# Reciprocal square roots of a single column on VectorE: a Newton step of two instructions with per-partition scalars instead of three

## The chip, the cores and the metric

The kernel runs on one core of one Trainium2 chip. Its engines work side by side from their own instruction queues: TensorE (PE, with its weight loads shown apart as PEld), VectorE (DVE), ScalarE (ACT), GpSimd (POOL) and SyncE (SP), which issues most of the transfers from memory. The metric is the device time of one execution in microseconds (us); lower is better.

## What is computed

The reference is a two-layer decoder trunk for 512 tokens of width 2048, in float32. Layer 0 is gated differential attention with 8 heads, layer 1 a gated RWKV-7 mixer. The change touches layer 0 alone, where each head normalises its attention output row by row:

```python
o = causal_diff_attention(q, k, v, lam)            # (B, T, 8 heads, 256)
o = rms_norm(o, subln_w) * (1.0 - lambda_init)     # y * rsqrt(mean(y*y) + 1e-6) over the 256
o = o.reshape(B, T, DA_WIDTH) * jax.nn.silu(gate)
return o @ w_out
```

The reciprocal root of that `rms_norm` is one number per token and head.

## The kernel before

Every large product is made of three float32r matmuls: each operand is split into a high part (a copy by ACT, `wh`) and a low part (a subtraction by DVE, `wl`), and `mm3` (its matmul is line 118) adds high*high, low*high and high*low. A weight block arrives by DMA in `wraw` (three buffers) or `T`; ACT casts one 128x512 slab of it (line 619) and DVE subtracts (line 620); four buffers hold the split slabs that PE reads. So PE, ACT and DVE form a pipeline that runs a few slabs ahead of the matmuls.

Layer 0 works head by head. While the projections of head h are multiplied (`Seven.head`), the attention of head h-1 runs as a `Chain`: a generator whose pieces are placed between the matmuls of the projection. For each block t of 128 tokens (four blocks a head) it has the pieces `scores`, `turn` (a transposition of the weights), `weigh` and `turn_y`. In `weigh`, PE makes the 128x256 output `o`; ACT squares and sums it into one column `so` (line 435); DVE adds epsilon (436), calls `rsqrt` with n = 1, multiplies the root `ro` with two other columns (439) and writes `y` (440), the normalised and gated 128x256 block. A fixed number of matmuls later PE transposes `y` into `yt` (`turn_y`, line 445), and ACT copies that to `yT` (line 449). PE's queue is in order: if `y` is not there by then, all matmuls behind wait.

`rsqrt` starts from the well-known integer estimate (two instructions, lines 63 and 64) and refines it with three Newton steps of three instructions each (lines 67, 68, 70). It is called 32 times with one column (8 heads x 4 blocks, line 438), and elsewhere with 2, 4, 8 or 16 columns.

Beside the chain, DVE has other work of the head in the same stretch: the rotary embedding of block t of the projected q and k (`rope`, lines 310 to 313, which overwrite the scratch tile `t2` that ACT's four squares of line 302 also write), and the sums of partial products (`take`, line 662). In the last pass it also splits rows of the finished attention for the output projection (lines 474 and 475).

The order of the instructions on every engine is set by a scheduler in the tile framework, from priorities that the code gives and the scheduler's own estimate of when each instruction can start. An instruction more or fewer can therefore change where its neighbours stand. Each engine then runs its list in order, and waits on semaphores where an operand is another instruction's result, also of the same engine.

Of the kernel before, what the change touches and what calls it, by code (L numbers as in the profile page):

```python
# [13 lines left out]
F32 = mybir.dt.float32  # L14
# [4 lines left out]
ALU = mybir.AluOpType  # L19
# [4 lines left out]
P = 128  # L24
# [33 lines left out]
def rsqrt(g, out, v, n, tag):  # L58

    nc = g.nc  # L60
    sh = g.small.tile([P, n], I32, name="rs_i", tag=tag + "i")
    t = g.small.tile([P, n], F32, name="rs_t", tag=tag + "t")
    nc.vector.tensor_single_scalar(sh[:], v.bitcast(I32), 1, ALU.logical_shift_right)
    nc.vector.tensor_scalar(sh[:], sh[:], -1.0, float(0x5F3759DF), ALU.mult, ALU.add)
    y = sh[:].bitcast(F32)
    for i in range(3):
        nc.vector.tensor_mul(t[:], y, y)
        nc.vector.scalar_tensor_tensor(t[:], t[:], -0.5, v, ALU.mult, ALU.mult)
        o = out if i == 2 else y
        nc.vector.scalar_tensor_tensor(o, t[:], 1.5, y, ALU.add, ALU.mult)  # L70
# [245 lines left out]
def norm_qk(g, q):  # L316

    nc, ss, rr = g.nc, q.ss, q.rr
    nc.vector.tensor_scalar(ss[:], ss[:], 1.0 / P, EPS, ALU.mult, ALU.add)
    rsqrt(g, rr[:].rearrange("p t c -> p (t c)"), ss[:].rearrange("p t c -> p (t c)"), 4 * NT, "r16")  # L320
    nc.vector.tensor_mul(rr[:], rr[:], g.rstd0[:, :, None].to_broadcast([P, NT, 4]))
    nc.vector.tensor_scalar(q.sq[:], rr[:, :, 0:2], P ** -0.5, None, ALU.mult)
    for t in range(NT):
        for c in (2, 3):
            cs = slice(c * P, (c + 1) * P)
            nc.scalar.activation(q.t1s[t][:, cs], q.t1s[t][:, cs], AF.Copy, scale=rr[:, t, c : c + 1])
# [57 lines left out]
def attention(g, h, qkT, qkL, sq, vg, gap, rows=None, yT=None):  # L384
# [42 lines left out]
    def weigh(t):  # L427
        b = blocks[t]
        o = g.ps.tile([P, 512], F32, name="o", tag="pc")
        for i in range(t + 1):  # L430
            bs = slice(i * P, (i + 1) * P)
            mm3(nc, o[:, :256], b.at[:, bs], b.al[:, bs], V[:, i, :], VL[:, i, :], i == 0, i == t)
        b.y = w.tile([P, 256], F32, name="y", tag="y", bufs=1)
        so = g.small.tile([P, 1], F32, name="so", tag="so")
        nc.scalar.activation(b.y[:], o[:, :256], AF.Square, scale=b.r[:, 0:1], accum_out=so[:])
        nc.vector.tensor_scalar(so[:], so[:], 1.0 / 256, EPS, ALU.mult, ALU.add)
        ro = g.small.tile([P, 1], F32, name="ro", tag="ro")
        rsqrt(g, ro[:], so[:], 1, "r1")
        nc.vector.scalar_tensor_tensor(ro[:], ro[:], b.r[:, 0:1], g.hrstd0[:, t : t + 1], ALU.mult, ALU.mult)
        nc.vector.scalar_tensor_tensor(b.y[:], o[:, :256], ro[:], G[:, t, :], ALU.mult, ALU.mult)  # L440
# [421 lines left out]
def layer0(g, aps):  # L862
# [3 lines left out]
    with ExitStack() as cx:  # L866
# [68 lines left out]
        g.rstd0 = g.const.tile([P, NT], F32, name="rstd0")  # L935
        g.hrstd0 = g.const.tile([P, NT], F32, name="hrstd0")
        rsqrt(g, g.rstd0[:], ss[:], NT, "r4")
        nc.vector.tensor_scalar(g.hrstd0[:], g.rstd0[:], 0.5, None, ALU.mult)
        with tc.issue_after(g.made[9][0]), tc.issue_after(g.made[9][1]):
# [937 lines left out]
```

## Time and profile before

| | |
|---|---|
| Time, median of 3 runs | 2086.14 us (2085.65 to 2088.14) |
| Time of the profiled execution | 2087.84 us |
| Its span, first to last instruction | 2086.1 us |
| PE busy | 2067.0 us (99%) |
| DVE busy | 1664.8 us (80%), 4353 instructions |
| ACT busy | 1250.9 us (60%) |
| POOL busy | 406.2 us (19%) |
| Attention of layer 0 beside the projections | about 125 to 790 us of the span |

A row of a timeline reads: start in us, duration in us, engine, line, operation, output<-inputs with their sizes, and in brackets how long the engine stood idle before and what ended that. Tile names leave their numbers out. A row of the groups reads: number of instructions, busy us in total, mean ns of one, and idle us before them. A matmul's row lasts longer than its place in the queue: rows of 128x512 start 0.23 us apart and last 0.39 us, since they are pipelined.

### The profile page before, as it was taken

What the parts mean: (1) busy time and instruction counts of PE and PEld (TensorE: products, weight loads), DVE (VectorE), ACT (ScalarE), POOL (GpSimd) and SP (SyncE); (2) the same over time, 40 slices, a digit from 0 to 9 for tenths busy, and PEclk for the clock granted to TensorE, in tenths of its full rate; (3) what the DMA queues carried; (4) which work ended last, traced back from release to release, by engine and by line L of the source; (5) the groups of instructions that cost most, each with busy time, mean ns of one, the idle gap of its engine ahead of it and who ended that gap; (6) DMA issues with size and microseconds to landing.
All of it is one profiled execution on the core that took longest, in us unless ns stands there. A gap on an engine that the chain in (4) does not pass through costs nothing.

```text
span 2086.1 us, 35354 instructions
## 1 busy us (share of the span) xinstructions
PE 2067.0 (99%) x12008; PEld 1708.6 (82%) x12008; DVE 1664.8 (80%) x4353; ACT 1250.9 (60%) x3005; POOL 406.2 (19%) x716
## 2 busy tenths in 40 slices
PE   9999999999999999999999999999999999999999
PEld 8888888888888888888778888888888888877887
DVE  5978778787877886576888888888888888887745
ACT  5766665666666664455666666666666666655333
POOL 0111011111111000101233332233333332342001
PEclk9999999999999999999999999999999999999999
DMA  6576777777777766742212222222222222235665
GB/s 200 146 181 178 182 187 190 181 193 180 190 175 192 182 222 196 169 118 93 79 64 79 80 78 69 82 79 82 76 79 79 79 79 74 89 126 166 204 163 120
DMA packets 101782, 280.71 MB, mean 135 GB/s; under 512 B 12545, under 2 KB 29073, under 8 KB 101601
## 3 DMA queue, kind: packets, MB, share of 16 engines
q1 hardware_dynamic: 68064, 198.90, 29.1%
q0 software_dynamic: 19104, 63.55, 16.4%
q10 hardware_dynamic: 14432, 16.01, 2.2%
q8 instruction: 94, 1.54, 0.3%
q14 instruction: 88, 0.71, 0.1%
HBM read 262.42 MB, written 15.99 MB: 133 GB/s over the span
## 4 chain that ended last, share of the span: by engine, by line
PE 92%; DVE 5%; ACT 2%; issue 1%; DMA 0%; POOL 0%; ACTq 0%; DVEq 0%; POOLq 0%
PE pp L118 70%; PE pt L118 6%; PE gp L1366 1%; PE sc L118 1%; PE sm L1585 1%; PE o L118 1%; PE sm L1607 1%; PE lora L118 1%; PE sm L1598 1%; PE z L118 1%; PE Y L1631 1%; DVE wl L110 1%; PE pt L359 1%; PE pt L1426 1%; PE px L1493 0%
## 5 line engine op out<-in xcount | busy, mean ns | idle before, releaser
L118 PE MATMUL pp<-hH,wh 128*128 128x512 f32 x1024 | 416.9, 407 | 0.0
L118 PE MATMUL pp<-hL,wh 128*128 128x512 f32 x1024 | 412.5, 403 | 0.0
L118 PE MATMUL pp<-hH,wl 128*128 128x512 f32 x1024 | 412.0, 402 | 0.0
L109 ACT CAST wh<-wraw 128x512 fp32r<-128x512 f32 (+1 forms) x412 | 253.8, 617 | 200.5 <-PE pp L118 103.5
L110 DVE TENSOR_TENSOR wl<-wraw,wh 128x512 fp32r<-128x512 f32 (+1 forms) x412 | 286.3, 696 | 102.6 <-ACT wh L109 98.7
L118 PE MATMUL pp<-wh,hH 128*128 128x512 f32 x932 | 366.5, 393 | 0.0
L118 PE MATMUL pp<-wh,hL 128*128 128x512 f32 x932 | 366.5, 393 | 0.0
L118 PE MATMUL pp<-wl,hH 128*128 128x512 f32 x932 | 364.4, 391 | 0.0
L118 PEld LDWEIGHTS pp<-hH,wh 128*128 128x128 f32 x1024 | 192.9, 188 | 37.6 <-issue 1.8
L118 PEld LDWEIGHTS pp<-hH,wl 128*128 128x128 f32 x1024 | 193.2, 189 | 32.8
L118 PEld LDWEIGHTS pp<-hL,wh 128*128 128x128 f32 x1024 | 193.3, 189 | 31.2
L118 PEld LDWEIGHTS pp<-wh,hL 128*128 128x128 f32 x932 | 175.1, 188 | 35.9
L118 PEld LDWEIGHTS pp<-wl,hH 128*128 128x128 f32 x932 | 175.2, 188 | 35.3 <-DVE wl L620 0.2
L118 PEld LDWEIGHTS pp<-wh,hH 128*128 128x128 f32 x932 | 175.3, 188 | 34.2
L620 DVE TENSOR_TENSOR wl<-wraw,wh 128x512 fp32r<-128x512 f32 x224 | 152.4, 688 | 60.0 <-ACT wh L619 59.4
L619 ACT CAST wh<-wraw 128x512 fp32r<-128x512 f32 x224 | 138.2, 620 | 93.8 <-PE pp L118 66.6
L1593 POOL COPY SA<-VS 64x64 f32<-64x64 f32 x224 | 75.1, 335 | 522.8 <-DVE VS L1611 466.4
L118 PE MATMUL pp<-wh,S 128*128 128x512 f32 x504 | 162.1, 395 | 0.0
L1459 DVE SCALAR_TENSOR_TENSOR tmpl<-LT,n,Tm 128x60 f32<-128x60 f32 (+24 forms) x496 | 135.6, 273 | 13.3
L582 POOL DMA_DIRECT2D T<-in_da_w_in_dram x63 | 53.7, 857 | 327.8 <-DVE wl L620 314.5
L1462 DVE TENSOR_TENSOR Tm<-Tm,tmpl 128x60 f32<-128x60 f32 (+24 forms) x496 | 106.2, 214 | 13.6
L619 ACT CAST wh<-T 128x512 fp32r<-128x512 f32 x126 | 77.8, 618 | 52.3 <-PE pp L118 52.2
(373 smaller groups left out, 3973.2 us busy)
## 6 DMA issues: line engine op xcount, KB each, us to landing
wraw<-in_rw_w_in_dram SPq DMA_DIRECT2D x128, 512.0 KB, 3.4
wraw<-in_da_w_in_dram SPq DMA_DIRECT2D x127, 512.0 KB, 4.3
T<-in_da_w_in_dram POOLq DMA_DIRECT2D x63, 512.0 KB, 6.1
wraw<-in_da_w_out_dram SPq DMA_DIRECT2D x26, 512.0 KB, 4.4
wraw<-in_rw_w_out_dram SPq DMA_DIRECT2D x26, 512.0 KB, 3.9
T<-in_da_w_in_dram SPq DMA_DIRECT2D x21, 512.0 KB, 4.3
wraw<-in_da_w_in_dram POOLq DMA_DIRECT2D x21, 512.0 KB, 6.9
yr<-yd SPq DMA_DIRECT2D x20, 256.0 KB, 3.1
```

Source lines behind the costliest of these rows:

```text
L109: nc.scalar.copy(hi[:], raw[:, k : k + n])
L110: g.split = nc.vector.tensor_sub(lo[:], raw[:, k : k + n], hi[:].bitcast(F32)).ins
L118: m = nc.tensor.matmul(out, a, b, start=s, stop=e, skip_group_check=skip)
L359: nc.tensor.transpose(pt[:, c * P : (c + 1) * P], t1s[t][:, c * P : (c + 1) * P], g.ident[:])
L582: self.g.nc.gpsimd.dma_start(out=raw, in_=src, accum_op=ALU.add)
L619: g.nc.scalar.copy(hi[:], raw[:, k])
L620: g.nc.vector.tensor_sub(lo[:], raw[:, k], hi[:].bitcast(F32))
L1366: m = nc.tensor.matmul(gp[h][:, i * P : (i + 1) * P], BK[r_, c0 + i, :, :], p.AR[r_, c0 + i, :, :], start=True, stop=True)
L1426: nc.tensor.transpose(ps[:, i * P : (i + 1) * P], p.BK[:, c0 + i].rearrange("p s t -> p (s t)"), g.ident[:])
L1459: st = nc.vector.scalar_tensor_tensor(tt, LT[:, i : i + 1, i + 1 :].to_broadcast([P, s, n]), n2[:, i : i + 1], Tm[:, 0:s, i : i + 1].to_br ...
L1462: nc.vector.tensor_add(Tm[:, 0:s, i + 1 :], Tm[:, 0:s, i + 1 :], tt)
L1593: nc.gpsimd.tensor_copy(p.SA[r_, c - 1, :], VS[r_, c, h, :])
```

## The change

For n = 1 `rsqrt` uses another form of the Newton step. Before, with estimate y of 1/sqrt(v): t = y*y; t = t*(-0.5)*v; y = (t+1.5)*y. Now h = -0.5*v is made once, and a step is t = (h*y)*y and y = (t+1.5)*y. The multiplication by y twice is one `tensor_scalar` whose two scalars are both the column y, read as one value per partition. A call has 2 + 1 + 3x2 = 9 instructions on DVE instead of 2 + 3x3 = 11. The scratch column becomes two columns wide. Calls with n > 1 are as before.

```diff
     sh = g.small.tile([P, n], I32, name="rs_i", tag=tag + "i")
-    t = g.small.tile([P, n], F32, name="rs_t", tag=tag + "t")
+    t = g.small.tile([P, max(n, 2)], F32, name="rs_t", tag=tag + "t")
     nc.vector.tensor_single_scalar(sh[:], v.bitcast(I32), 1, ALU.logical_shift_right)
     nc.vector.tensor_scalar(sh[:], sh[:], -1.0, float(0x5F3759DF), ALU.mult, ALU.add)
     y = sh[:].bitcast(F32)
-    for i in range(3):
+    if n == 1:
+        t, h = t[:, 0:1], t[:, 1:2]
+        nc.vector.tensor_single_scalar(h, v, -0.5, ALU.mult)
+    for i in range(3) if n == 1 else ():
+        nc.vector.tensor_scalar(t, h, y, y, ALU.mult, ALU.mult)
+        nc.vector.scalar_tensor_tensor(out if i == 2 else y, t, 1.5, y, ALU.add, ALU.mult)
+    for i in range(3) if n > 1 else ():
         nc.vector.tensor_mul(t[:], y, y)
         nc.vector.scalar_tensor_tensor(t[:], t[:], -0.5, v, ALU.mult, ALU.mult)
         o = out if i == 2 else y
```

In the changed kernel the new lines are 68 (h), 70 (t) and 71 (y); every later line of the old kernel has a number higher by 6. The scheduler also places some neighbours otherwise. Three places, first before and then now.

DVE, the end of the last block of a head (the sixth attention head; the second to the sixth have the same order). `rs_t` and `rs_i` are t and y, `wl` a weight slab's low part, `t1<-pp,u` the sums of `take`, `t2<-t1,ropeS` the first product of the rotary embedding.

```order
L68 SCALAR_TENSOR_TENSOR rs_t_6913<-rs_t_6913,so_6908 128x1
L662 TENSOR_TENSOR t1_6290<-pp_1234,u_1238 128x512
L70 SCALAR_TENSOR_TENSOR rs_i_6912<-rs_t_6913,rs_i_6912 128x1
L662 TENSOR_TENSOR t1_6291<-pp_1235,u_1239 128x512
L67 TENSOR_TENSOR rs_t_6913<-rs_i_6912 128x1
L620 TENSOR_TENSOR wl_7004<-wraw_6996,wh_7003 128x512
L68 SCALAR_TENSOR_TENSOR rs_t_6913<-rs_t_6913,so_6908 128x1
L620 TENSOR_TENSOR wl_7030<-wraw_7026,wh_7029 128x512
L70 SCALAR_TENSOR_TENSOR ro_6911<-rs_t_6913,rs_i_6912 128x1
L439 SCALAR_TENSOR_TENSOR ro_6911<-ro_6911,r_6742,hrstd0_596 128x1
L310 TENSOR_TENSOR t2_7049<-t1_6290,ropeS_637 128x4x64
L440 SCALAR_TENSOR_TENSOR y_6907<-o_6894,ro_6911,G_6267 128x256
```

```order
L668 TENSOR_TENSOR t1_6251<-pp_1235,u_1239 128x512
L70 TENSOR_SCALAR rs_t_6867<-rs_t_6867,rs_i_6866 128x1
L626 TENSOR_TENSOR wl_6952<-wraw_6948,wh_6951 128x512
L71 SCALAR_TENSOR_TENSOR rs_i_6866<-rs_t_6867,rs_i_6866 128x1
L626 TENSOR_TENSOR wl_6956<-wraw_6948,wh_6955 128x512
L70 TENSOR_SCALAR rs_t_6867<-rs_t_6867,rs_i_6866 128x1
L626 TENSOR_TENSOR wl_6982<-wraw_6978,wh_6981 128x512
L71 SCALAR_TENSOR_TENSOR ro_6865<-rs_t_6867,rs_i_6866 128x1
L316 TENSOR_TENSOR t2_7001<-t1_6250,ropeS_637 128x4x64
L445 SCALAR_TENSOR_TENSOR ro_6865<-ro_6865,r_6698,hrstd0_596 128x1
L626 TENSOR_TENSOR wl_6986<-wraw_6978,wh_6985 128x512
L446 SCALAR_TENSOR_TENSOR y_6861<-o_6848,ro_6865,G_6227 128x256
```

Between the row `so` and the row `y` of this block there stood four `wl`; now there are five, the fifth right ahead of `y` (in the first head there are four before and now). The rotary row `t1<-t1,t2` (line 313), which stood ahead of `so`, now stands behind it, and the small instructions stand apart from each other, with a large one between most of them.

ACT, a little earlier in the same block. `t2,ss<-t1` are the squares of one 128x512 block in four parts, `yT` the copy of the block before after its transposition, `wh` a slab's high part.

```order
L619 CAST wh_6934<-T_715 128x512
L302 ACTIVATE t2_6962,ss_6293<-t1_6289,rstd0_595 128x128 x2
L619 CAST wh_6976<-wraw_6973 128x512
L302 ACTIVATE t2_6962,ss_6293<-t1_6289,rstd0_595 128x128
L449 ACTIVATE yT_6890<-yt_6887,subw_693 128x128 x2
L451 DMA yd_78<-yT_6890 128x2x128
```

```order
L625 CAST wh_6886<-T_715 128x512
L308 ACTIVATE t2_6914,ss_6253<-t1_6249,rstd0_595 128x128 x2
L625 CAST wh_6928<-wraw_6925 128x512
L308 ACTIVATE t2_6914,ss_6253<-t1_6249,rstd0_595 128x128
L455 ACTIVATE yT_6844<-yt_6841,subw_693 128x128 x2
L308 ACTIVATE t2_6914,ss_6253<-t1_6249,rstd0_595 128x128
```

The fourth square stood ahead of the copies to `yT`; now it stands behind them.

PE, the last block of the seventh attention head (the last one that runs beside a projection). `yt` is the transposition of `y`; the others are matmuls of the projection with the slab `wh`, `wl`.

```order
L118 MATMUL pp_1233<-wl_8001,S1_707 128x512
L118 MATMUL pp_1233<-wh_8000,S1_707 128x512
L118 MATMUL pp_1232<-wh_8026,S1_708 128x512
L118 MATMUL pp_1232<-wl_8027,S1_708 128x512
L118 MATMUL pp_1232<-wh_8026,S1_708 128x512
L445 MATMUL yt_8014<-ident_82,y_7907 128x128 x2
L118 MATMUL pp_1233<-wh_8026,S1_708 128x512
L118 MATMUL pp_1233<-wl_8027,S1_708 128x512
L118 MATMUL pp_1233<-wh_8026,S1_708 128x512
```

```order
L124 MATMUL pp_1233<-wl_7945,S1_707 128x512
L124 MATMUL pp_1233<-wh_7944,S1_707 128x512
L451 MATMUL yt_7958<-ident_82,y_7853 128x128 x2
L124 MATMUL pp_1232<-wh_7970,S1_708 128x512
L124 MATMUL pp_1232<-wl_7971,S1_708 128x512
L124 MATMUL pp_1232<-wh_7970,S1_708 128x512
L124 MATMUL pp_1233<-wh_7970,S1_708 128x512
L124 MATMUL pp_1233<-wl_7971,S1_708 128x512
```

The transposition stands three matmuls further ahead than before. Elsewhere PE's list has only a few more moves, of one to five places, all within some hundred rows behind this one. In SP's list two transfers of that stretch move by a few rows and two change places; POOL's list is the same.

## The prediction

> **What bounds the kernel now.** I read the page's first part, then busy time by stretch, then who PE waited for. First the page's shares: PE is busy 99% of the span, DVE 80%.
>
> ```profile
> PE 2067.0 (99%) x12008; PEld 1708.6 (82%) x12008; DVE 1664.8 (80%) x4353; ACT 1250.9 (60%) x3005; POOL 406.2 (19%) x716
> ```
>
> An average hides stages, so here are two stretches of 90 us in the attention, where the 32 calls lie. The columns are the length, then busy time and instructions of PE, PEld, DVE, ACT and POOL, then granted clock, DMA share and GB/s.
>
> ```profile
> 580.00:670.00 90.00, 89.41 (x432) 74.43 (x431) 70.77 (x196) 56.90 (x144) 11.07 (x15) 1.00 0.75 184
> 670.00:760.00 90.00, 88.80 (x429) 73.19 (x428) 74.84 (x214) 59.64 (x153) 5.87 (x7) 1.00 0.69 197
> ```
>
> PE stands idle 0.59 and 1.20 us in them, DVE 19 and 15 us. A few DVE instructions fewer can only shorten the time where PE waits for DVE. The waits of PE that fall into the attention are these (total us, times, longest):
>
> ```profile
> PE pt L359 <- DVE qkL L363: 1.2, 3, 0.6
> PE pt L359 <- ACT t L326: 0.7, 1, 0.7
> PE yt L445 <- DVE y L440: 0.6, 1, 0.6
> PE pt L421 <- DVE p L415: 0.3, 1, 0.3
> PE pp L118 <- DVE wl L620: 0.2, 1, 0.2
> ```
>
> Together they are 3.0 us (0.14% of the span), and of the 32 `yt` that follow a call of this root, one waited for its `y`. That is most of what this change could win. What it could lose depends on how late `y` may come in the other 31.
>
> **The cost of the instructions.** These groups hold the one-column instructions (number, then busy us, mean ns):
>
> ```profile
> L68 DVE SCALAR_TENSOR_TENSOR rs_t<-rs_t,so 128x1 f32<-128x1 f32 x96 | 15.0, 156 | 1.5
> L67 DVE TENSOR_TENSOR rs_t<-rs_i 128x1 f32<-128x1 f32 x96 | 14.9, 155 | 1.6
> L70 DVE SCALAR_TENSOR_TENSOR rs_i<-rs_t,rs_i 128x1 f32<-128x1 f32 x64 | 10.0, 156 | 1.2
> L439 DVE SCALAR_TENSOR_TENSOR ro<-ro,r,hrstd 128x1 f32<-128x1 f32 x32 | 7.0, 218 | 1.0
> L64 DVE TENSOR_SCALAR rs_i<-rs_i 128x1 int32<-128x1 int32 x32 | 4.8, 151 | 0.6
> ```
>
> Removed are the 96 of line 67 and the 96 of line 68, 29.9 us. Added are 32 for h, a `tensor_scalar` with a constant as line 64 is: 32 x 151 ns = 4.8 us; and 96 of the new t. No row shows a `tensor_scalar` with two columns as scalars. From below it costs what one with constants does, 151 ns. Line 439 reads one scalar from a column and takes 218 ns against 156 for line 68, 62 more; twice that on 151 is 275 ns, the upper end. I take 218, since line 439 is the nearest row: 96 x 218 = 20.9 us. DVE's busy time then changes by 4.8 + 20.9 - 29.9 = -4.2 us (ends -10.6 and +1.3). None of it is on the path by itself, since DVE's other work and PE's matmuls cover it; what counts is when each `y` is there.
>
> **Where y is nearly late.** DVE at the last block of the sixth head:
>
> ```profile
> 617.75 0.42 DVE L310 TENSOR_TENSOR t<-t,ropeS 128x256 f32<-128x256 f32 x1
> ...
> 620.06 0.15 DVE L63 TENSOR_SCALAR rs_i<-so 128x1 int32<-128x1 int32 x1
> 620.13 0.68 DVE L620 TENSOR_TENSOR wl<-wraw,wh 128x512 fp32r<-128x512 f32 x1
> 620.73 0.15 DVE L64 TENSOR_SCALAR rs_i<-rs_i 128x1 int32<-128x1 int32 x1
> 620.91 0.16 DVE L67 TENSOR_TENSOR rs_t<-rs_i 128x1 f32<-128x1 f32 x1
> 621.10 0.16 DVE L68 SCALAR_TENSOR_TENSOR rs_t<-rs_t,so 128x1 f32<-128x1 f32 x1
> ...
> 622.25 0.68 DVE L662 TENSOR_TENSOR t<-pp,u 128x512 f32<-128x512 f32 x1
> 622.85 0.15 DVE L70 SCALAR_TENSOR_TENSOR rs_i<-rs_t,rs_i 128x1 f32<-128x1 f32 x1
> ...
> 625.19 0.22 DVE L439 SCALAR_TENSOR_TENSOR ro<-ro,r,hrstd 128x1 f32<-128x1 f32 x1
> 625.33 0.42 DVE L310 TENSOR_TENSOR t<-t,ropeS 128x256 f32<-128x256 f32 x1
> 625.66 0.48 DVE L440 SCALAR_TENSOR_TENSOR y<-o,ro,G 128x256 f32<-128x256 f32 x1
> ```
>
> Three distances between starts are to be read here. A small instruction whose operand is the previous one's result starts 0.19 us after it (620.91 to 621.10). One with an independent neighbour behind it costs only 0.07 us (620.06 to 620.13), and 0.14 if it reads a scalar from a column (625.19 to 625.33). A large one takes 0.60 (622.25 to 622.85), a rotary product 0.33. The rows of PE for this block, and for the block before and the seventh head's last:
>
> ```profile
> 616.75 0.38 PE L445 MATMUL yt<-ident,y 128*128 128x128 f32 x2
> ...
> 621.61 0.39 PE L118 MATMUL pp<-wh,hL 128*128 128x512 f32 x1
> ...
> 626.82 0.38 PE L445 MATMUL yt<-ident,y 128*128 128x128 f32 x2
> ...
> 719.37 0.39 PE L118 MATMUL pp<-wl,S 128*128 128x512 f32 x1
> 719.59 0.39 PE L118 MATMUL pp<-wh,S 128*128 128x512 f32 x1
> 720.55 0.44 PE L445 MATMUL yt<-ident,y 128*128 128x128 f32 x2 [0.57 <-DVE y L440]
> ```
>
> In the sixth head `y` ends at 625.66 + 0.48 = 626.14 and PE takes it at 626.82: 0.68 us to spare, of which a `yt` that did wait shows about 0.06 to be hand-over (the seventh head's `y` ends at 720.49, below, and PE starts at 720.55).
>
> **Heads two to six, last block.** The new order puts one more `wl` ahead of `y` (+0.60) and the rows of ACT move: the fourth square now follows the two copies to `yT`, and rotary line 310 waits for all four.
>
> ```profile
> 617.02 0.40 ACT L302 ACTIVATE t<-t,rstd 128x128 f32<-128x128 f32 x1
> ...
> 617.41 0.60 ACT L449 ACTIVATE yT<-yt,subw 128x128 f32<-128x128 f32 x2
> ...
> 634.41 1.14 ACT L619 CAST wh<-wraw 128x512 fp32r<-128x512 f32 x2 [2.68 <-DMA wraw<-in_da_w_in_dram]
> 637.26 0.62 ACT L619 CAST wh<-wraw 128x512 fp32r<-128x512 f32 x1 [1.71 <-PE pp L118]
> ```
>
> `yt` of the block before is made at 616.75, so the copies run from about 617.1 to 617.7 and the square to 618.3: line 310 starts some 0.6 later than 617.75, at 618.35. From there I lay the new list out with the distances above (an estimate). Lines 310 to 312, `so`, 313, the second estimate row and h, and the first `wl`: to 621.2. Then t and the first sum of `take`, which may start once PE's group has ended (its last matmul for the other half starts at 621.61): 621.55; with the next small one and the second sum to 622.8. The second t (0.14), two `wl` with a small one each, the third t (0.14): 624.35. A `wl` (0.60), the last y, line 310, line 439 and the fifth `wl`: 626.2. `y` then ends at 626.7, against 626.82: about 0.1 to spare, 0.04 beyond the hand-over. Cost: 0, with little room. If the new t takes 0.33 instead of 0.14 (the ends further down), the two late ones add 0.4, and PE waits some 0.35 in each of five heads, 1.7 us. In the first head four `wl` stand there before and now, so nothing is lost.
>
> **Third blocks.** There `y` ends at 616.23 (row below) for a `yt` at 616.75, 0.52 to spare, as many large instructions stand ahead as before, and dependent neighbours are pulled apart: no cost. The first two blocks have the same kind of order and did not wait: no cost.
>
> ```profile
> 615.75 0.48 DVE L440 SCALAR_TENSOR_TENSOR y<-o,ro,G 128x256 f32<-128x256 f32 x1
> ```
>
> **Seventh head, last block.** Here PE waits today, and the new list has five `wl` ahead of `y` instead of six, one row split (line 475) less and no line 311 there, while 313 comes in behind `so`:
>
> ```profile
> 719.28 0.22 DVE L439 SCALAR_TENSOR_TENSOR ro<-ro,r,hrstd 128x1 f32<-128x1 f32 x1
> 719.41 0.69 DVE L620 TENSOR_TENSOR wl<-wraw,wh 128x512 fp32r<-128x512 f32 x1
> 720.01 0.48 DVE L440 SCALAR_TENSOR_TENSOR y<-o,ro,G 128x256 f32<-128x256 f32 x1
> ```
>
> That is 0.60 + 0.60 + 0.33 = 1.5 us less, and 0.6 more at the start for ACT's later square, so `y` ends near 719.6. PE asks three matmuls earlier than before, 3 x 0.23 = 0.7 us ahead of 719.98 (720.55 less its wait), at 719.3. A wait of 0.3 remains where there was 0.57, and the 0.2 us that PE waited for a `wl` goes with it, because that `wl` no longer stands behind two row splits. Gain 0.5 us. If `y` is a row split later than I think, it turns into a loss of 0.1 us.
>
> **Last head.** It runs beside the output projection, and its chain is exposed:
>
> ```profile
> 785.17 0.22 DVE L439 SCALAR_TENSOR_TENSOR ro<-ro,r,hrstd 128x1 f32<-128x1 f32 x1
> 785.50 0.48 DVE L440 SCALAR_TENSOR_TENSOR y<-o,ro,G 128x256 f32<-128x256 f32 x1
> ```
>
> None of its four `yt` waits now, and the chain gets shorter or stays: nothing. The 0.33 us from 785.17 to 785.50 are the longest distance that a column-scalar row has before a row that needs it, and the upper end for the new t.
>
> The Trainium skill ("VectorE: DVE Perf Modes", section "The DRAIN you can't avoid") says that a semaphore after each of eight copies cost nothing extra: 13.88 us with and without. For one-column instructions this trace differs, 0.19 us against 0.07. By the page the new t would cost 0.14 everywhere and the 1.7 us of the upper end would fall away; by the rows they stay possible.
>
> **Sum.** 0 (31 blocks) - 0.5 (seventh head) = -0.5 us on a span of 2086.1, 2085.6, and 2087.3 for the profiled execution. That execution's 2087.84 lies 1.7 above the median of the runs, so against the median 2086.14 the forecast is 2085.6 us: no change that shows. A difference of 0.2% (4.2 us) is about what a measurement of this kernel can tell; the three runs alone span 2.5 us.
>
> **The rivals.**
>
> *Slower: late weights.* In the new list the second `wl` of that block comes 1.2 to 1.4 us later than before, and it frees a buffer of `wraw` for the next transfer. If the weights land that much later and PE has no reserve, five heads lose up to 1.4 us each, 7 us: 2092.6. For it: ACT did wait 2.68 us for such a transfer at 634.41. Against it: its next slab waited for PE to free a buffer until 637.26, so the slabs were over 2 us ahead of PE there. It decides once the delay passes that reserve. 8%; with the upper price of t and other shifts of the order together some 12% for slower by over 0.2%.
>
> *The change doesn't do what it says: t costs 275 ns and holds the next instruction 0.33.* DVE then is not relieved (+1.3 us) and `y` comes late in five heads: +1.7 - 0.5 = +1.2, 2087.3. One column scalar cost 62 ns more than none, which speaks for it; the 0.14 to an independent neighbour speaks against it. 22%, within 0.2%.
>
> *Faster: DVE's relief reaches PE.* If the looser order also ended the other waits of PE listed above, all 3.0 us would go: 2083.1. They hang on `qkL`, t of line 326 and p, whose rows ahead hardly change. 12%, within 0.2%; to pass 4.2 us, hidden gaps between matmuls would have to close too, for which 0.23 us from matmul to matmul leaves little. 7%.
>
> *My forecast*, -0.5 us with nothing new on PE's path: 47%. So faster 0.07, same 0.81, slower 0.12. The range goes from the floor of 2083.1 less the scatter of the lower runs (0.5) to the second rival plus the scatter of the upper one (2.0): 2082.6 to 2089.3. The 2092.6 is left out.
>
> **What would show it.** Right: DVE has 64 instructions fewer and about 4 us less busy; the new t lasts near 218 ns; `y` of the last block of heads two to six ends some 0.1 us before its `yt`; the seventh head's wait for `y` is halved; PE is busy as before. Wrong: PE's list of waits shows `yt` <- `y` five times or more, or waits of PE for `wl` behind a late transfer; or t lasts 0.3 us or more.

## The result, and the profile of the changed kernel

The changed kernel takes 2090.25 us (median of 22 runs, 2086.50 to 2093.64), the kernel before 2086.86 us beside it (22 runs): a ratio of 1.0014, with a 95% interval of 1.0007 to 1.0020. It is slower by some 3 us, where 0.5 us less was forecast. Four runs among those used below, one each of e2, e8, e11 and the kernel before on the third chip, took 2133 us or more, and all medians and ratios leave them out. The profiled execution of the changed kernel took 2093.64 us, so it is the slowest of its 22, with a span of 2091.7 us.

The page's first part, then busy time in the two stretches of the attention that the prediction shows, then the waits of PE in the attention (total us, times, longest):

```profile
PE 2070.0 (99%) x12008; PEld 1708.1 (82%) x12008; DVE 1663.8 (80%) x4289; ACT 1252.4 (60%) x3005; POOL 406.1 (19%) x716
```

```profile
580.00:670.00 90.00, 89.26 (x430) 74.19 (x429) 70.93 (x191) 56.86 (x143) 11.42 (x15) 1.00 0.76 183
670.00:760.00 90.00, 88.33 (x426) 72.53 (x425) 74.22 (x198) 60.21 (x151) 5.68 (x7) 1.00 0.70 196
```

```profile
PE pt L365 <- DVE qkL L369: 3.0, 5, 1.0
...
PE pt L427 <- DVE p L421: 1.0, 1, 1.0
```

DVE has its 64 instructions fewer, but PE gets less done: 430 and 426 matmuls in the two stretches instead of 432 and 429. The wait that has grown is not the one for `y`. It is the wait of the keys' transposition (`pt`, line 365) for `qkL` (line 369), from 1.2 us in three heads to 3.0 in five; the wait for p in the last head has grown from 0.3 to 1.0.

The groups of the new instructions and the end of the sixth head's last block on DVE, with PE's row for it:

```profile
L70 DVE TENSOR_SCALAR rs_t<-rs_t,rs_i 128x1 f32<-128x1 f32 x96 | 25.9, 270 | 1.6
L68 DVE TENSOR_SCALAR rs_t<-so 128x1 f32<-128x1 f32 x32 | 4.6, 144 | 0.0
```

```profile
627.53 0.27 DVE L70 TENSOR_SCALAR rs_t<-rs_t,rs_i 128x1 f32<-128x1 f32 x1
627.72 0.68 DVE L626 TENSOR_TENSOR wl<-wraw,wh 128x512 fp32r<-128x512 f32 x1
...
629.45 0.48 DVE L446 SCALAR_TENSOR_TENSOR y<-o,ro,G 128x256 f32<-128x256 f32 x1
```

Then PE's two matmuls ahead of this `yt`, in the kernel before (its `yt`, at 626.82, is in the prediction) and in the changed one:

```profile
626.37 0.62 PE L118 MATMUL pp<-wh,S 128*128 128x512 f32 x2
```

```profile
629.46 0.61 PE L124 MATMUL pp<-wh,S 128*128 128x512 f32 x2
629.99 0.44 PE L451 MATMUL yt<-ident,y 128*128 128x128 f32 x2
```

The new t lasts 0.27 us and holds an independent neighbour 0.19 us (627.53 to 627.72). `y` ends at 629.93 and PE takes it at 629.99, which is the hand-over and nothing more: PE was ready a little earlier. From the start of these two matmuls to `yt` it takes 0.53 us where it took 0.45. With the matmul behind, about 0.1 us is lost at the last `yt` of each of heads two to six, 0.5 us together. Each of these waits is too short to stand in the list of waits.

**Where the time went.** The path from the weights to `pt`, in the sixth head, before and after. The rows are of POOL (its copy `on` marks that a transfer to `wraw` has landed), DVE, ACT and PE; ACT's row for the landed pair of slabs in the kernel before is in the prediction (634.41). `pt` is PE's transposition of the scaled q and k; the work that leads to it is called the keys' path below. First the kernel before:

```profile
624.29 0.18 POOL L602 COPY on<-wraw 128x1 f32<-128x1 f32 x1 [17.19 <-DMA wraw<-in_da_w_in_dram]
...
635.07 1.29 DVE L620 TENSOR_TENSOR wl<-wraw,wh 128x512 fp32r<-128x512 f32 x2 [1.58 <-ACT wh L619]
636.28 0.42 DVE L310 TENSOR_TENSOR t<-t,ropeS 128x256 f32<-128x256 f32 x1
...
641.18 2.46 ACT L326 ACTIVATE t<-t,rr 128x128 f32<-128x128 f32 x8 [1.93 <-DVE rr L321]
...
646.22 0.63 PE L359 MATMUL pt<-ident,t 128*128 128x128 f32 x4 [0.59 <-DVE qkL L363]
```

And the changed kernel:

```profile
628.32 0.52 POOL L608 COPY on<-wraw 128x1 f32<-128x1 f32 x1 [17.31 <-DMA wraw<-in_da_w_in_dram]
...
634.43 0.41 ACT L308 ACTIVATE t<-t,rstd 128x128 f32<-128x128 f32 x1
...
637.79 1.14 ACT L625 CAST wh<-wraw 128x512 fp32r<-128x512 f32 x2 [2.87 <-DMA wraw<-in_da_w_in_dram]
...
638.45 1.29 DVE L626 TENSOR_TENSOR wl<-wraw,wh 128x512 fp32r<-128x512 f32 x2 [1.74 <-ACT wh L625]
639.66 0.42 DVE L316 TENSOR_TENSOR t<-t,ropeS 128x256 f32<-128x256 f32 x1
...
644.56 2.45 ACT L332 ACTIVATE t<-t,rr 128x128 f32<-128x128 f32 x8 [2.09 <-DVE rr L327]
...
649.59 0.63 PE L365 MATMUL pt<-ident,t 128*128 128x128 f32 x4 [0.74 <-DVE qkL L369]
```

A pair of weight slabs lands late. ACT casts it at once, DVE makes its two low parts, and behind these two in DVE's list stands the rotary embedding of the head's last block. All that it waits for is there long before (the last square ends at 634.84), but DVE works in order: from the late pair to line 316 it is 1.2 us, to the scaling by rr 6.1, and then come the transposition, its copy, `qkL` and PE. So what a transfer is late, the keys are late.

In the table, both columns of a kernel are counted from the last `yt` of the head (626.82 and 629.99 here): the start of ACT's cast of the late pair, and the start of the second group of `pt`, each from the rows of the trace.

| head | before: pair, pt | after: pair, pt | before, moved (e9) | after, moved (e10) |
|---|---|---|---|---|
| 2 | 7.46, 19.25 | 7.75, 19.55 | 5.93, 18.64 | 7.05, 18.68 |
| 3 | 6.88, 18.67 | 7.31, 19.10 | 7.56, 18.64 | 6.51, 18.70 |
| 4 | 6.32, 18.65 | 7.98, 19.78 | 7.68, 18.64 | 6.88, 18.69 |
| 5 | 6.76, 18.64 | 7.42, 19.22 | 7.08, 18.65 | 7.68, 18.70 |
| 6 | 7.59, 19.40 | 7.80, 19.60 | 6.92, 18.65 | 7.90, 18.69 |

In the two kernels themselves `pt` starts at 18.65 us, plus whatever the pair is later than 6.85 (7.98 - 6.85 = 1.13, and 18.65 + 1.13 = 19.78). Before, the pair came at 7.00 on average, just about that point; after, at 7.65. The delays of `pt` behind 18.65 add up to 1.4 us before and 4.0 after. (The last two columns are those of the experiments.)

The spans differ by 5.6 us, and the trace divides them so: 2.6 us in these five heads; 1.0 from the seventh head's last `yt` to the last head's (66.55 to 68.23 us, less the 0.7 by which the three matmuls' earlier place makes it longer), where the wait for p is; 0.5 in other places of the first seven heads; and 1.5 behind the last `yt` of the attention (1299.0 to 1300.5), where the granted clock was lower in this execution:

```profile
core 0: 2091.7 us, clock 0.998
```

PE's lists of the two kernels are alike but for a few moves, so their rows can be laid side by side, and PE's lag be read from matmul to matmul. That divides the 0.5: 0.4 us gained in the first 30 us of the program (seven of the eleven later profiles gain 0.3 us or more there too), 0.6 lost in the first head, 0.5 lost at the five `yt` above, and 0.2 gained at the seventh head's. In the first head PE waits for a low part of late weights, which the kernel before doesn't:

```profile
180.96 0.50 PE L124 MATMUL pp<-wl,hH 128*128 128x512 f32 x1 [0.24 <-DVE wl L626]
```

For the kernel before the clock was 0.999. What of the difference is the kernel's and what the clock's is among the questions below.

### The profile page after: what moved, and what is told of

Read it like the earlier page. It is cut to its first block, busy times and chain, and to the rows that moved or that the text cites. A ratio compares the mean times of both kernels' runs of the same rounds, so it can differ in the third digit from the quotient of the medians.

```text
span 2091.7 us, 35289 instructions
## 1 busy us (share of the span) xinstructions
PE 2070.0 (99%) x12008; PEld 1708.1 (82%) x12008; DVE 1663.8 (80%) x4289; ACT 1252.4 (60%) x3005; POOL 406.1 (19%) x716
## 4 chain that ended last, share of the span: by engine, by line
PE 90%; DVE 5%; ACT 2%; issue 1%; DMA 1%; POOL 0%; ACTq 0%; DVEq 0%; POOLq 0%
PE pp L124 69%; PE pt L124 6%; PE sc L124 1%; PE gp L1372 1%; PE o L124 1%; PE sm L1591 1%; PE sm L1613 1%; PE lora L124 1%; PE sm L1604 1%; DVE wl L116 1%; PE Y L1637 1%; DMA wraw<-in_da_w_in_dram 1%; PE pt L365 1%; PE pt L1432 1%; PE z L124 1%
## 5 line engine op out<-in xcount | busy, mean ns | idle before, releaser
L124 PEld LDWEIGHTS pp<-wh,S 128*128 128x128 f32 x504 | 93.2, 188 | 17.8
```

The costliest lines, as they stand in the source:

```text
L124: m = nc.tensor.matmul(out, a, b, start=s, stop=e, skip_group_check=skip)
```

## The experiments

The theories: A, the order. ACT's fourth square stands behind the `yT` copies, so the rotary row 316 and all behind it on DVE are late, buffers come free late, the pair lands late and the keys with it. B, the price of the new t, 0.27 us instead of 0.16, in itself. C, the clock. All medians are of 11 runs (10 of e2 and e11, 6 of e8), beside the kernel before on the same chip: e1 to e4 on one (before 2087.01 us), e5 to e8 on a second (2086.29), e9 to e11 on a third (2086.88).

**e1: the fourth square put back ahead of the copies, in the changed kernel.**

```diff
...
+        if t == 1 and c == 3 and getattr(g, "yTs", None):
+            for x in g.yTs:          # the two copies to yT
+                g.tc.add_manual_dep(x, i_.ins.name, ...)   # only an order
...
```

> The changed kernel with one rule of order added: ACT does the fourth square of the second rotary block ahead of the two copies to yT, as in the kernel before. Theory A (the order did it: square behind the copies, so the rotary rows, the weight splits and the transfers behind them come later, and the late pair of weights holds up the keys' path to qkL): the five waits of PE for qkL fall from 3.0 us to about the 1.2 us of the kernel before, and the time from 2090.2 to about 2087 us. Theory B (the price of the new t, 0.27 us each, three a call): the instructions are the same, so it stays near 2090 us.

2087.91 us, 1.0005 (0.9996 to 1.0014). PE's wait for `qkL` is gone from its list, the pair comes at 6.80 on average, and the delays of `pt` are 0.3 us together. That is most of the loss back with the new t in place: for A, against B. `y` has 0.5 to 0.8 us to spare again, too, so this run doesn't tell the two gains apart.

**e2: the other way round, the fourth square put behind the copies in the kernel before.**

```diff
+        with (g.tc.issue_after(g.yTs[-1]) if t == 1 and c == 3 and getattr(g, "yTs", None)
+              else ExitStack()):
...
```

> The kernel before, three instructions a Newton step, with one rule of order added: the fourth square of the second rotary block stands behind the two copies to yT. Theory A: the pair of weights lands later, PE waits some 3 us for qkL, and the time is about 2089 to 2090 us though no instruction is changed. Theory B: no new t in it, so 2086.9 us.

2088.35 us, 1.0008 (0.9999 to 1.0017): less than the 2089 to 2090 of A, more than the 2086.9 of B. The profile is of the fastest run (2085.77). Its waits of PE in the attention:

```profile
PE yt L447 <- DVE y L442: 0.9, 1, 0.9
PE pt L423 <- DVE p L417: 0.5, 1, 0.5
PE pt L361 <- ACT t L328: 0.2, 1, 0.2
```

No wait for `qkL`, where A had some 3 us, and the pair came early, at 5.6 to 6.4. The interval holds 1. So the square alone doesn't bring the pair late; for the first link of A (from the order to the landing) this run is a miss. What the square does cost here is `y`: in heads two to six it ends 0.06 us ahead of its `yt`, and PE loses 0.2 us at each, 1 us together.

**e3 and e10: one move in the changed kernel.** The late pair's two low parts are put behind the last rotary row. PE's list stays as it is, and in ACT's two rows of the seventh head move to later places, by three and by five.

```diff
-    nc.vector.tensor_add(t1[:], t1[:], t2[:])
+    return nc.vector.tensor_add(t1[:], t1[:], t2[:]).ins
...
-                g.nc.vector.tensor_sub(lo[:], raw[:, k], hi[:].bitcast(F32))
+                with g.tc.issue_after(after) if after else ExitStack():
+                    g.nc.vector.tensor_sub(lo[:], raw[:, k], hi[:].bitcast(F32))
...
-            ws = self.split(raw)
+            ws = self.split(raw, self.roped if last and k > 2 * KP else None)
...
-            rope(g, q, t)
+            self.roped = rope(g, q, t)
```

> The changed kernel, with the rotary rows of the last block placed on DVE ahead of the late pair of weight splits instead of behind it; nothing else moves. Theory A: the path to qkL no longer hangs on the pair's landing, the waits of PE for qkL nearly go (below 0.5 us from 3.0), and the time falls by about 3 us to 2087 us, though the weights land as late as in the changed kernel. Theory B: 2090 us.

> The changed kernel with the same single move, beside the next run on one chip. Theory A (the landing of the late pair sets the keys' path): 2.0 to 3.0 us less than the changed kernel, and on each of five heads the scaling of t by rr starts 12.7 us after yt wherever the pair lands. Theory B (the price of t): no difference to the changed kernel beyond 0.5 us.

2087.51 us (1.0002, 0.9993 to 1.0011) and 2087.09 us (1.0002, 0.9994 to 1.0011). On the second of these chips the changed kernel itself took 2090.61 (e11), so one move, of two instructions in a head, gives back 3.5 us of 3.7, somewhat more than the 2.0 to 3.0 expected. The sixth head of e10, whose last `yt` starts at 626.81, on ACT, DVE and PE:

```profile
634.71 1.15 ACT L625 CAST wh<-wraw 128x512 fp32r<-128x512 f32 x2 [2.97 <-DMA wraw<-in_da_w_in_dram]
...
633.42 0.42 DVE L316 TENSOR_TENSOR t<-t,ropeS 128x256 f32<-128x256 f32 x1
...
635.55 1.29 DVE L627 TENSOR_TENSOR wl<-wraw,wh 128x512 fp32r<-128x512 f32 x2
...
639.52 2.45 ACT L332 ACTIVATE t<-t,rr 128x128 f32<-128x128 f32 x8 [0.25 <-DVE rr L327]
...
645.50 0.60 PE L365 MATMUL pt<-ident,t 128*128 128x128 f32 x4
```

The pair is as late as ever (7.90 after `yt`), but the rotary rows are done, and the scaling starts 12.71 after `yt`, in all five heads 12.71 to 12.74. PE waits for no `qkL`. The last column of the table above is this run.

**e4 and e9: the same move in the kernel before.**

> The kernel before with the same move as the run above: the rotary rows of the last block ahead of the late pair of weight splits. Theory A: its waits for qkL (1.2 us) go, so about 2085.7 us against 2086.9. Theory B says nothing of it: 2086.9 us.

> The kernel before with the late weight pair's low parts behind the last rotary row, once more: does it beat the kernel before? The waits for qkL that it takes away were 1.2 us in the kernel before's profile, so theory A: 1.0 to 1.6 us less, 0.9992 to 0.9995. If the first result was chance: within 0.3 us of the kernel before.

2085.44 us (0.9992, 0.9983 to 1.0001) and 2085.45 us (0.9990, 0.9981 to 0.9999). The scaling starts 12.67 to 12.77 after `yt` although the pair comes anywhere from 5.88 to 7.81. The second interval lies below 1, the first just holds it. On the third chip this is 1.4 us below the kernel before, as much as that one's profile has of delays at `pt`, and 5.2 below the changed one. With the move in both, the changed order is still slower, by 1.6 us (e10 against e9) and 2.1 us (e3 against e4). The two profiles of the third chip, laid side by side, show e10 losing 0.8 us in the first head, 0.5 at the five `yt` and 0.7 in the last two heads. So the late pair isn't the whole loss.

**e6 and e11: the changed kernel once more.**

> The changed kernel unchanged, beside the kernel before and the next two on one chip. Theory A (order: ACT's fourth square behind the yT copies makes rotary line 316 late, the late weight pair late behind it in DVE's queue, and the keys' transposition later still): 2089 to 2090.5, 1.0010 to 1.0015, with PE waiting 1 to 3 us for qkL. Theory C (the chip of the first measurement dipped its clock more often under this kernel): 2087 to 2088, 1.0005 at most, since on the other chip a median over equal clocks remains.

> The changed kernel itself, for the comparison with the two runs above: 1.0010 to 1.0015 of the kernel before, as on the two other chips.

2089.72 us (1.0013, 1.0004 to 1.0021) and 2090.61 us (1.0017, 1.0007 to 1.0026; a little above what was expected). In the runs whose mean granted clock was 1.00, the medians on the third chip are 2086.13 for the kernel before (9 runs), 2089.05 for the changed one (3), 2086.53 for e10 (5) and 2084.56 for e9 (5); on the second they are 2085.75 before (15) and 2087.91 after (4). So C doesn't make the difference, of which 2.2 to 2.9 us are left at the full clock; it widened the one between the two profiles.

The landing scatters from execution to execution: the delays of `pt` sum to 2.9 us in e6 and 1.9 in e11, against 4.0 in the first profile. Their mean of 2.9, less the 1.4 of the one profile of the kernel before, makes 1.5 of the 3.4 to 3.7 us. That one profile isn't an odd one: the landings of e4 and e9 would give 1.5 and 1.8 by the rule of 6.85 (an estimate). By the same count e10 takes 2.7 us of delays away, where 3.5 were measured. Laid side by side with the kernel before, the three profiles of the changed kernel lose on average 0.5 us in the first head, 1.9 in heads two to six (the delays, and 0.5 at the five `yt`) and 0.6 in the last two, where the wait for p is 0.3 to 1.2: 3.0 of the 3.4 to 3.7 us. An interval of 0.09% to either side is 1.9 us, so the rest can't be told from noise. The move shows what the late pair costs; the other parts are read from traces alone.

**e5: both rules in the changed kernel** (the diffs of e1 and e3 together).

> The changed kernel with both rules together: ACT's fourth square ahead of the yT copies, and the late weight pair's low parts behind the last rotary row. Theory A: both causes are gone; no wait of PE for qkL, 2085.5 to 2087, at or below the kernel before. Theory B (the price of the new t, 0.27 us, is what costs): the t is in it as before, 2089 to 2090. If the wait for p in the last head stays at 0.9 us, that much of the loss is apart from both.

2086.49 us, 1.0001 (0.9992 to 1.0009), 3.2 us under the changed kernel on the same chip. `y` has 0.5 to 0.8 us to spare again in the last blocks of heads two to six. One wait of PE is left in the attention, with its cause in DVE's list behind it:

```profile
PE pt L431 <- DVE p L425: 1.7, 1, 1.7
```

```profile
749.67 0.69 DVE L116 TENSOR_TENSOR wl<-wraw,wh 128x512 fp32r<-128x512 f32 x1 [1.26 <-ACT wh L115]
750.28 0.15 DVE L414 SCALAR_TENSOR_TENSOR nb<-mx,sq 128x1 f32<-128x1 f32 x1
```

The column `nb`, which the softmax of the last head's first block needs, stands behind a low part that waits 1.26 us for its high part: the same pattern at another place. With the t of 0.27 us in it, this kernel is level with the one before. The fair comparison is with e4, which has the move as well: laid side by side, the two are equal to 0.1 us from the first head to the sixth, and e5 loses 1.2 us in the last two, mostly by this wait. So B costs nothing that shows in six heads; whether the new t has a part in this wait isn't shown.

**e7: the same arithmetic with two instructions more in a call.** t is multiplied by 1.0 in the first two steps, so a call has eleven instructions again; the scheduler then leaves the fourth square ahead of the copies and puts four `wl` ahead of `y`.

```diff
         nc.vector.tensor_scalar(t, h, y, y, ALU.mult, ALU.mult)
+        if i < 2:
+            nc.vector.tensor_single_scalar(t, t, 1.0, ALU.mult)
```

> The changed kernel with a multiplication of t by 1.0 in the first two Newton steps: eleven one-column instructions in a call as before the change, the new t as it is, and ACT's fourth square again ahead of the yT copies, with four low parts ahead of y. Theory A: 2086 to 2087.5, no wait for qkL in the middle heads, although DVE gets 64 instructions more (64 x 0.15 = 9.6 us busier than after). Theory B: the chain of each call is 2 x 0.19 us longer and t as dear, so 2090 to 2093.

2089.22 us, 1.0016 (1.0007 to 1.0025): A expected 2086 to 2087.5 and was wrong in this form, and the 2090 to 2093 of B was missed from the other side. The profile is of the slowest run (2093.28). PE's waits in the attention, and DVE's rows of one call:

```profile
PE pt L367 <- DVE qkL L371: 2.1, 3, 1.2
PE pt L429 <- DVE p L423: 1.9, 1, 1.9
PE yt L453 <- DVE y L448: 1.2, 2, 1.0
```

```profile
530.84 0.27 DVE L70 TENSOR_SCALAR rs_t<-rs_t,rs_i 128x1 f32<-128x1 f32 x1
531.15 0.15 DVE L72 TENSOR_SCALAR rs_t<-rs_t 128x1 f32<-128x1 f32 x1
...
532.02 0.27 DVE L70 TENSOR_SCALAR rs_t<-rs_t,rs_i 128x1 f32<-128x1 f32 x1
532.21 0.68 DVE L670 TENSOR_TENSOR t<-pp,u 128x512 f32<-128x512 f32 x1
```

The square is in its old place, and yet the pair comes at 7.04, 7.41, 6.22, 7.52 and 8.22, and `pt` at 18.84, 19.20, 18.65, 19.31 and 20.02, on the line of the table. So the place of the square isn't the cause in itself. What differs here is that the pair's own transfer is issued 0.2 us behind `yt`, where the kernel before issues it right at `yt`. This run tells the second link of A (the landing to the keys) from the first, and only the second holds in all of them.

**e8: t as (y*h)*y in one `scalar_tensor_tensor`, with one column as scalar.**

```diff
-        nc.vector.tensor_scalar(t, h, y, y, ALU.mult, ALU.mult)
+        nc.vector.scalar_tensor_tensor(t, y, h, y, ALU.mult, ALU.mult)
```

> The changed kernel with t = (y*h)*y as one scalar_tensor_tensor with one column as scalar in place of tensor_scalar with two. Price of t: 0.22 us by the row of ro (one column scalar), against 0.27 now; DVE's busy time 96 x 0.05 = 4.8 us less. The order moves much more (three low parts ahead of y in the last block, ACT's square still behind the yT copies). Theory A: some late weights remain, 2088 to 2091. Theory B: cheaper t, 2086 to 2088.

2093.06 us, 1.0036 (1.0022 to 1.0050): the slowest of all, with the cheapest t, above the 2088 to 2091 of A as well as the 2086 to 2088 of B. The profile is of the slowest of the six runs (2101.77). The group of t, and PE's largest wait in the attention:

```profile
L70 DVE SCALAR_TENSOR_TENSOR rs_t<-rs_i,rs_t 128x1 f32<-128x1 f32 x96 | 20.7, 215 | 1.4
```

```profile
PE pt L365 <- ACT t L332: 9.8, 5, 2.3
```

t takes 215 ns, and `y` has 1.7 us to spare in the last blocks. But the scheduler puts the rotary rows of two blocks, not one, behind the late pair. In the fifth head:

```profile
554.16 1.29 DVE L626 TENSOR_TENSOR wl<-wraw,wh 128x512 fp32r<-128x512 f32 x2 [1.92 <-ACT wh L625]
555.37 0.42 DVE L316 TENSOR_TENSOR t<-t,ropeS 128x256 f32<-128x256 f32 x1
...
559.88 0.42 DVE L316 TENSOR_TENSOR t<-t,ropeS 128x256 f32<-128x256 f32 x1
```

The scaling by rr starts at 567.53, 13.4 us behind the pair's low parts instead of 6.1, and PE waits in five heads. That is the same path from a late pair to `pt`, with more rows in it, and the opposite of what B expects.

## Why the prediction was wrong

The step that failed is the cost of 0 for the last blocks of heads two to six (second point below). The first head, the price of t and the gain at the seventh head were wrong in size besides.

- *The price of t.* 0.22 us were taken, 0.27 measured (the upper end was 0.275). To an independent neighbour it holds 0.19 us, not 0.14 and not 0.33. With h, 30.5 us were added for 29.9 removed; DVE's busy time fell by 1.0 us in all, not by 4.2. Mis-sized, but inside the ends, and e5 shows no cost of it in the first six heads. The Trainium skill ("VectorE: DVE Perf Modes", section "The DRAIN you can't avoid") has a semaphore behind each of eight copies cost nothing extra. e7 differs: 0.31 us from t to the row that needs it (530.84 to 531.15), 0.19 to one that doesn't.
- *Heads two to six, last block.* The step that failed is the end of this working, "Cost: 0, with little room", which became the 0 of 31 blocks in the sum. It followed ACT's later square and the additional `wl` only as far as `y` and PE's `yt`, and not to the rows behind. What the runs show in place of the 0: the keys' path behind the late pair, whose delays in these five heads rise from 1.4 us to 2.9 on average in three profiles, and which e3 and e10 take away by moving the pair's low parts. For `y` itself about 0.1 us to spare was forecast, 0.04 of it beyond the hand-over; measured is the hand-over alone (0.06) and a loss of 0.1 us in each head. That is a good forecast of the time of `y`, but on the wrong side of the edge: 0.5 us in five heads.
- *First head.* "So nothing is lost" went by the number of `wl`. The weights land later there too (ACT casts the late slab 2.75 us after `yt`, 1.83 before), and PE waits 0.24 us for its low part in the first profile, 0.62 in e11 and not at all in e6. The loss is 0.5 us on average.
- *Third blocks.* 0.52 us to spare was taken, 0.67 measured (`y` to `yt`): no cost, right.
- *Seventh head.* A gain of 0.5 us was forecast. The wait for `y` is 0.6 as before, with `yt` asked three matmuls (0.7 us) earlier; two of the `wl` there now wait 0.29 and 0.35 us for ACT, which the estimate from distances between starts didn't contain. PE gains 0.1 to 0.2 us at this `yt` and loses as much at the next `pt`. The wait for p, a little later, took 0.3 to 1.2 us in three profiles of the changed kernel, against 0.3: no gain, and in two of three a loss.
- *The rival "late weights".* It had the right transfer and the right sign, and was set at 8% for the wrong consumer. Its mechanism, a buffer that comes free later, doesn't hold for the pair's own transfer, which is issued earlier (below). Against it stood that PE's next slab was over 2 us ahead; in heads two to six that is so, and PE waits for no slab there (in the first head it does, see above). But DVE's list carries the slab's low parts and the keys' rotary rows in one order. The row quoted for the rival (2.68 us of ACT's idle time for the transfer, at 634.41) was the head of the path that already cost PE 0.59 us in that very head.
- *The rival "faster".* It dismissed the waits for `qkL` with "whose rows ahead hardly change". The rows hardly change, but the time of the first of them does, by the transfer. This sentence is where the prediction could have been right: the list of PE's waits named `qkL` first, with 1.2 of 3.0 us, and the wait wasn't followed back to what it hung on. (Of the 3.0 us, the 0.7 for t of line 326 lie at 90 us, ahead of the stretch in which the 32 calls are, so this rival's 2083.1 was 0.7 too low.)

The in-order behaviour of DVE's list is read from 634.43 and 639.66 above: the rotary row, which writes the tile that the squares wrote, starts 4.8 us after the last square has ended. The Trainium skill says so too ("DVE: scalar operands, raw-bit mode, write accounting and state across instructions", section "Flops that outlive an instruction": the DVE's queue is one in-order queue), and the trace agrees. Its rule to minimise the number of chained operations on this engine ("VectorE: DVE Perf Modes", section "Rules for kernel authors") doesn't carry here: 64 fewer are 3.4 to 3.7 us slower, 64 put back in e7 are no better, and two instructions moved make up for it.

What stays open: why the pair lands later after the change. Its own transfer is not issued later. These are SyncE's rows of it in the sixth head, first before, then after:

```profile
626.77 0.33 SPq L584 DMA_DIRECT2D wraw<-in_da_w_in_dram  x1
```

```profile
629.56 0.33 SPq L590 DMA_DIRECT2D wraw<-in_da_w_in_dram  x1
```

Against `yt` (626.82, 629.99) that is 0.05 us ahead before and 0.43 after, so it is issued earlier and takes longer: on average of the five heads 6.9 us before and 8.0 after. For this transfer, A's "buffers come free late" is refuted. Late is the block's first transfer: it is issued 5.95 us ahead of `yt` before and 5.44 after, and lands later (624.29 against 626.82 before, 628.32 against 629.99 after: 2.5 us ahead of `yt`, then 1.7). POOL's accumulating transfer, which waits for it, starts 1.84 us ahead of `yt` before and 1.21 after, and in all five heads after the change the pair lands 0.2 us behind that one. The groups of transfers (median us from issue to landing last) show the accumulating ones 0.4 us longer, first before, then after:

```profile
T<-in_da_w_in_dram POOLq DMA_DIRECT2D x63, 512.0 KB, 6.1
...
wraw<-in_da_w_in_dram POOLq DMA_DIRECT2D x21, 512.0 KB, 6.9
```

```profile
T<-in_da_w_in_dram POOLq DMA_DIRECT2D x63, 512.0 KB, 6.5
...
wraw<-in_da_w_in_dram POOLq DMA_DIRECT2D x21, 512.0 KB, 7.3
```

That transfers in flight at the same time hold each other up would fit this, and e2 too: there the pair is issued 0.42 us ahead of `yt` as in the changed kernel, but POOL's transfer starts 2.01 ahead, and the pair lands at 5.8 us on average instead of 7.6. e8 fits it less well (0.47 and 1.50 ahead, and it lands at 7.7, the latest of all). No run here changes one of the two alone.

## What to carry to other kernels

Where PE is the bound, an edit to another engine is worth what it does to the waits of PE that already exist, so follow each of them back to its first cause, through the queues, before pricing the edited instructions. Work that waits for a transfer should stand behind, not ahead of, independent work on an in-order engine: moving two such instructions in a head was worth 1.4 us in the kernel before and 3.5 in the changed one, where the shorter root took 1.0 us off DVE's busy time and nothing off the kernel's. And where a scheduler sets the order, a change in the number of small instructions is a change of order: judge it by the order it gives, and repeat it with the order held.

## What the runs showed of the hardware

- A 128x1 `tensor_scalar` with two columns as scalars takes 270 ns, a `tensor_scalar` with a constant 144 ns; a `scalar_tensor_tensor` with one column as scalar 215 ns (e8), one with a constant 156 ns (line 68 before): some 60 ns for each column scalar.
- The same weight transfer at the same place of the program lands up to 1.9 us apart from head to head in one execution (5.88 to 7.81 us after `yt` in e4), and this scatter shows in the time only where something on PE's path stands behind it.
